# An eight-head hybrid attention block on one NeuronCore: half the search budget while splitting, another opening of attention, loads issued a job ahead

## The chip, the core and the metric

The kernel runs on one core of a Trainium2 chip. The metric is the device time of one execution in microseconds (us). TensorE is called PE here, its weight loads PEld, VectorE DVE, ScalarE ACT, GpSimd POOL and SyncE SP. Each engine runs its own list of instructions in order, and waits where an instruction needs something that another engine or a transfer has not delivered yet. All transfers (DMA) of this kernel are issued by SP, in the order of SP's list.

## The reference

One layer with 2048 positions and a width of 1024, in float32:

```python
xn = rms_norm(x, norm_gain)
proj = xn @ w_in                 # split into the inputs of both branches
# branch A: 8 heads of 64; a chunk of 64 sees itself and 8 chunks before it
yA = softmax(qc @ kc.T * scale + bias) @ vc * silu(gateA)
# branch B: 8 heads of 64 on one shared key and value; per block of 128 queries
score = sum_h relu(iq_h @ ik.T) * iw_h       # 8 indexer heads of 32
idx = top_k(score, 256)                       # among admissible keys
yB = softmax(q @ k[idx].T * scale) @ v[idx] * silu(gateB)
merged = sigmoid(gA) * (yA @ w_branch_a) + sigmoid(gB) * (yB @ w_branch_b)
out = rms_norm(x + merged @ w_out, final_norm_gain)
```

## The kernel before

Products of float32 matrices are made of three matmuls (`mm3`, L216): both operands are split into a high and a low part, and high x high, high x low and low x high are added up. So each product also costs splits: ACT writes the high part, DVE or POOL subtracts it to get the low part.

The program runs in these stages.

- **Scaling and index projection** (0 to about 100 us). x is normalized, and the inputs of the indexer are made. For two of the four groups of 512 positions the scaling runs later, beside the projection: `norm_early` loads two tiles (`xs`, and for one group `xa`), scales them on ACT and POOL and stores them.
- **Projection** (to about 1060 us). A list of `jobs` takes one piece of weights and one group of positions each. A job is two or four chains of 24 matmuls into a PSUM tile `acc`. The weights' splits (`wt`, L207 and L208) are made by ACT and POOL, the evacuations by ACT and DVE. The second half of the positions is finished by quarter products of sums of blocks, whose prepared weights come from `prep_full`.
- **Search** (within the projection, to 753 us). For branch B the positions' top 256 keys are found by thresholds, in order to get masks (`mskD`). `logits()` makes the scores of a block of 128 queries: a matmul into a buffer `lg` (L478), Relu on ACT (L480), weighted sum on DVE into `sc` (L485). `search()` finds the threshold of a pair of blocks by counting on DVE and ACT. Both are threads that yield with a cost in ns. After each chain of the projection `tick(x)` lets them run for `rate * x` ns, where the rate is one of `PUMP` and `PUMP2`. While `again` holds work that splits the second half's input, x is `TQ` or 0.35 instead of 1 or 0.5. When the threads have ended, `close_search` calls `search_again`: it counts the blocks whose count is off into `bad` (L577), adds that up on PE (L580) and makes a flag (L582), on which DVE and POOL branch. Then the pools of the sums are opened, and `again` gets their loads.
- **Attention** (about 1050 to 1885 us). A unit of branch A, `a_unit(G, h)`, is one head for a group of 512 queries; a unit of branch B, `b_unit(b, u)`, is two heads of block b. Each has loads, a first part (scores `s` on PE, L905 and L1014, maximum `mx` on DVE, L831, exponential on ACT, L909 and L1017) and a second part (transposes `pt` on PE, their split `pth` and `ptl`, product `O`). `attention()` runs the second part of a unit in turns with the first part of the next, and issues loads two units ahead. `seq` is the order of the units; it is made before by a rule that compares the shares of both branches' costs (`CA_`, `CB_`) that are done. `kv_at` says at which unit keys and values of a group of branch B (`kBt`, `vBt`) are loaded, and `extra` when the products `d` with `w_branch_a` and `w_branch_b` are made (`branch`).
- **Output product** `po` (L1420) to the end at 2087 us.

A scheduler that estimates times orders the instructions of each engine when the program is built, so a change of a rate or of the order of units moves instructions on all engines. The order that it made is fixed at run time.

## Time and profile before

| what | before |
|---|---|
| runs | 2090.68, 2093.07, 2093.47 us; median 2093.07 |
| profiled execution | 2089.03 us, span 2087.2 us |
| busy share | PE 96%, PEld 81%, DVE 71%, ACT 62%, POOL 39% |
| mean granted clock of PE | 0.987 |
| PE busy in 0 to 60 us | 49.21 of 60 |
| PE busy in 60 to 120 us | 47.49 of 60 |
| PE busy in 1060 to 1120 us | 43.68 of 60 |
| PE busy in 2040 to 2087 us | 38.87 of 47 |

Times of windows and rows are microseconds from the start of the span. A row of an instruction has its start, its length, engine, line and operation, output and inputs with partitions and elements, and in brackets how long the engine stood idle before it and what ended that. A row of a group has busy time, mean length in ns and idle time before it with its releasers. In a row of the table of waits stand the waiting and the releasing group. A granted clock of 1.00 is full speed.

### The profile page before, as it was taken

The numbers are of one execution on the slowest core, as the hardware profiler recorded it, in microseconds if no ns is written. First come the engines' busy times: TensorE is split into PE (matmuls) and PEld (weight loads), VectorE is DVE, ScalarE is ACT, GpSimd is POOL, SyncE is SP. The second block draws the span as 40 slices with busy tenths as digits, with TensorE's granted clock in tenths as the row PEclk, the third lists the DMA queues.
The fourth block names the chain that finished last, engine by engine and source line by source line (L and its number), as shares of the span: only waits on it lengthen the run. The fifth ranks groups of instructions, "written<-read, shape, count | busy, mean of one in ns | idle before, by whom it ended". The sixth has DMA issues, their size and how long they took to land.

```text
span 2087.2 us, 33654 instructions
## 1 busy us (share of the span) xinstructions
PE 1997.9 (96%) x10706; PEld 1693.9 (81%) x10706; DVE 1475.8 (71%) x3746; ACT 1285.5 (62%) x2644; POOL 809.9 (39%) x981
## 2 busy tenths in 40 slices
PE   8798999999998999999978999999999999999998
PEld 7576888889888887888867888888888888888886
DVE  6739899989798836555546678766886688865434
ACT  5465666656565544654458779866886688873221
POOL 2146322122221345545435455445444644343410
PEclk9899999999999999999989999999999999999999
DMA  9487433354545453333485664555245631145642
GB/s 359 145 290 242 166 131 123 106 176 147 178 170 175 150 184 112 116 129 119 134 237 171 203 192 143 155 177 191 88 124 178 195 109 51 58 140 191 216 134 91
DMA packets 225928, 333.77 MB, mean 160 GB/s; under 512 B 28625, under 2 KB 99665, under 8 KB 225617
## 3 DMA queue, kind: packets, MB, share of 16 engines
q1 hardware_dynamic: 225744, 331.57, 49.2%
q8 instruction: 85, 1.39, 0.3%
q14 instruction: 99, 0.80, 0.1%
HBM read 219.33 MB, written 112.16 MB: 159 GB/s over the span
## 4 chain that ended last, share of the span: by engine, by line
PE 53%; DMA 4%; DVE 2%; ACT 2%; issue 1%; POOL 1%; SPq 1%; DVEq 0%; ACTq 0%; POOLq 0%
PE acc L216 12%; PE po L1420 9%; PE d L216 8%; PE O L1039 6%; PE s L1014 5%; PE pt L1031 5%; PE O L949 3%; PE s L905 3%; PE pt L939 3%; DMA dst<-wA 1%; DMA kk<-kA 1%; DMA dst<-wB 1%; DVE P L831 1%; DMA ost<-wO 1%; DVE ptl L855 0%
## 5 line engine op out<-in xcount | busy, mean ns | idle before, releaser
L216 PE MATMUL acc<-xh,wt 128*128 128x512 f32 x1856 | 599.3, 394 | 5.7 <-DVE e L336 2.4
L216 PEld LDWEIGHTS acc<-xh,wt 128*128 128x128 f32 x1856 | 347.2, 188 | 84.4 <-DVE e L336 2.6
L216 PE MATMUL acc<-xl,wt 128*128 128x512 f32 x928 | 363.8, 393 | 0.0
L208 POOL TENSOR_TENSOR wt<-wst,wt 128x512 fp32r<-128x512 f32 (+1 forms) x108 | 145.4, 1375 | 419.8 <-ACT wt L207 303.4
L852 POOL TENSOR_TENSOR ptl<-pf,pth 128x512 fp32r<-128x512 f32 (+1 forms) x144 | 179.6, 1247 | 178.0 <-ACT pf L848 128.4
L855 DVE TENSOR_TENSOR ptl<-pt,pth 128x512 fp32r<-128x512 f32 (+1 forms) x288 | 187.3, 660 | 45.0 <-ACT pth L854 42.5
L216 PEld LDWEIGHTS acc<-xl,wt 128*128 128x128 f32 x928 | 174.5, 188 | 38.7
L485 DVE SCALAR_TENSOR_TENSOR sc<-lg,iw,sc 128x512 f32<-128x512 f32 (+2 forms) x266 | 178.6, 678 | 26.1 <-ACT lg L480 21.9
L1014 PE MATMUL s<-kBt,qsB 128*128 128x512 f32 (+3 forms) x640 | 188.0, 385 | 1.3 <-DVE mx L831 0.9
L480 ACT ACTIVATE lg<-lg 128x512 f32<-128x512 f32 (+2 forms) x304 | 147.9, 521 | 44.5 <-PE lg L478 43.6
L854 ACT ACTIVATE pth<-pt 128x512 fp32r<-128x512 f32 (+1 forms) x288 | 159.3, 578 | 25.2 <-PE pt L939 11.5
L1017 ACT ACTIVATE P<-P,mx 128x128 f32<-128x128 f32 (+15 forms) x128 | 154.3, 1207 | 20.6 <-DVE mx L831 20.1
L1031 PE MATMUL pt<-ident,P 128*128 128x128 f32 x1088 | 164.4, 273 | 1.2 <-DVE ptl L855 0.6
L1039 PE MATMUL O<-pth,vBt 128*128 128x256 f32 x544 | 146.3, 288 | 3.2 <-ACT pth L854 1.4
L1039 PE MATMUL O<-ptl,vBt 128*128 128x256 f32 x544 | 145.8, 295 | 1.8 <-POOL ptl L852 1.2
L831 DVE CUSTOM_DVE_ANT_0 P<-s,mk,mx 128x512 f32<-128x512 f32 (+2 forms) x192 | 125.0, 651 | 29.8 <-PE s L1014 24.7
L1031 PEld LDWEIGHTS pt<-ident,P 128*128 128x128 f32 x1088 | 127.0, 140 | 10.5 <-DVE ptl L855 1.1
L1077 POOL TENSOR_TENSOR dw<-dst,dw 128x512 fp32r<-128x512 f32 x64 | 82.7, 1292 | 124.5 <-ACT dw L1076 122.7
L478 PE MATMUL lg<-ikT,iqT 128*128 128x512 f32 (+2 forms) x304 | 111.3, 378 | 18.0 <-DVE sc L485 17.9
L905 PE MATMUL s<-kk,qz 128*128 128x256 f32 (+2 forms) x464 | 113.8, 341 | 15.4 <-DMA kk<-kA 7.8
L533 ACT ACTIVATE jk<-sc,st 128x640 int8<-128x640 f32 (+6 forms) x49 | 71.2, 1453 | 84.3 <-DVE st L551 73.6
L1014 PEld LDWEIGHTS s<-kBt,qsB 128*128 128x128 f32 x640 | 102.9, 190 | 15.8 <-DVE mx L831 9.1
(286 smaller groups left out, 4738.9 us busy)
## 6 DMA issues: line engine op xcount, KB each, us to landing
wst<-wP SPq DMA_DIRECT2D x100, 256.0 KB
wst<-wS SPq DMA_DIRECT2D x56, 256.0 KB
kk<-kA SPq DMA_DIRECT2D x56, 256.0 KB
vs<-vA SPq DMA_DIRECT2D x56, 256.0 KB
qz<-qA SPq DMA_DIRECT2D x96, 128.0 KB
xrow<-x SPq DMA_DIRECT2D x16, 512.0 KB
vA<-eh SPq DMA_DIRECT2D x32, 256.0 KB
dst<-wA SPq DMA_DIRECT2D x32, 256.0 KB
```

What stands on the lines that cost most here:

```text
L216: nc.tensor.matmul(acc, a, b, start=(first and i == 0), stop=(last and i == n - 1), **({} if first and last else {"skip_group_check": True}))
L480: nc.scalar.activation(lg, lg, AF.Relu)
L485: nc.vector.scalar_tensor_tensor(o_, lg, wv, o_, op0=OP.mult, op1=OP.add)
L852: nc.gpsimd.tensor_tensor(lo, pf, f32(hi), op=OP.subtract)
L854: nc.scalar.activation(hi, src, AF.Copy)
L855: nc.vector.tensor_tensor(lo, src, f32(hi), op=OP.subtract)
L905: nc.tensor.matmul(s_ps[:, :w], q[:, m, j * 128:(j + 1) * 128], kk[:, ko:ko + w], start=(m == 0), stop=(m == 1))
L1014: nc.tensor.matmul(s_ps[:, :w], q[:, h, :], kBt[:, m, a:a + w], start=(m == 0), stop=(m == 1))
L1017: nc.scalar.activation(P[:, e, :n], P[:, e, :n], AF.Exp, bias=mx[:, e:e + 1], scale=-1.0, accum_out=st["sum"][:, (u % 2) * 2 + e:(u % 2) * ...
L1031: nc.tensor.transpose(pt[:, k, e, :], P[:, e, (kt + k) * 128:(kt + k + 1) * 128], ident)
L1039: nc.tensor.matmul(o_, vBt[:, kt + k, :], src[:, k, :], start=(kt + k == 0 and n_ == 0), stop=(kt + k == b and n_ == 1), skip_group_check= ...
L1420: nc.tensor.matmul(accs[t, hf], a, b[:, n_], start=(k == 0 and i == 0), stop=(k == KT - 1 and i == 2))
```

## The change

- The search's budget for each chain while `again` holds work falls from 0.75 to 0.5 (`TQ`) and from 0.35 to 0.25; a score of one column costs 1.25 instead of 1.11 in the threads' account; `PUMP2` rises from 9000 to 11000.
- The loads of `norm_early` go into a function of their own, `load_early`, which is called a job ahead; the first of them is at job 8 instead of 6 (`EN0`).
- Attention starts with three units of branch A's first group; the other five are mixed with blocks 4 to 7 of branch B, then blocks 0 to 3 come, then 8 to 15 (`LEAD`, `GB`, `C0_`). The new order is A0.0 A0.1 A0.2 b4.0 A0.3 b4.1 A0.4 b4.2 A0.5 b4.3 b5.0 A0.6 b5.1 A0.7 b5.2 A1.0 and so on; the end is the same. Keys and values of groups 0 and 1 are loaded at the first unit, and the small copies on POOL that hold a load back (`GATE`) are made for groups 2 and 3 alone.
- The three bias tiles of heads `NB` and above are loaded behind the first unit instead of in `open_late`.
- `open_early` opens the pool `dna` ahead of `wp_`, which gives their tiles other addresses.

```diff
--- before.py
+++ after.py
@@ -38,14 +38,15 @@
 ROUNDS = 2
 SGB, TYB = 1, 1
 BLOCKS = [2, 4, 5, 6, 7, 8, 9, 10, 11, 12, 13, 14, 15, 3]
-PUMP, PUMP2 = (5300, 4500), 9000
+PUMP, PUMP2 = (5300, 4500), 11000
 DVE_KINDS = ("qb", "va", "ka", "qa")
-EN0, TQ = 6, 0.75
+EN0, TQ = 8, 0.5
 SQD = (2,)
 FIRST = (2, 4)
 SB, HB = 2, 3
 WK, WAT = 5, 1
-SPL, LEAD = 96, 8
+SPL, LEAD = 96, 3
+GB, C0_ = (1, 0, 2, 3), 14
 CA_, CB_, TAILB = 26, 9, 260
 NEWTON, HALVES = 3, 2
 GATE, OFF = 1, 60.0
@@ -483,7 +484,7 @@
                             nc.vector.tensor_scalar(o_, lg, wv, 0.0, op0=OP.mult, op1=OP.add)
                         else:
                             nc.vector.scalar_tensor_tensor(o_, lg, wv, o_, op0=OP.mult, op1=OP.add)
-                        yield 120 + w * 1.11
+                        yield 120 + w * 1.25
             nc.vector.memset(sc[0:64, n - 64:n], OUT)
             nc.sync.dma_start(scD[b, :, :n], sc[:, :n])
             scores[b] = sc[:, :n]
@@ -780,8 +781,8 @@
     def open_early():
 
         nonlocal sml, wk, wy, wz, dna, wp_, pe
+        dna = dph.enter_context(pool("dna", side="right"))
         wp_ = dph.enter_context(pool("wp_", side="right"))
-        dna = dph.enter_context(pool("dna", side="right"))
         sml = ph.enter_context(pool("sml", bufs=4, side="right"))
         wk = ph.enter_context(pool("wk", bufs=2, side="right"))
         wy = ph.enter_context(pool("wy", bufs=2, side="right"))
@@ -800,7 +801,6 @@
         kBt = att.tile([128, 2, S], F32R, name="kBt")
         vBt = att.tile([128, NT, 128], F32R, name="vBt")
         mk01 = att.tile([128, 2, 256], BF16, name="mk01")
-        load_bias(range(NB, H), att)
         nc.vector.memset(mk01, 0.0)
         nc.vector.memset(mk01[0:64, 0, 64:128], FAR)
         nc.vector.memset(mk01[0:64, 1, 192:256], FAR)
@@ -1095,12 +1095,11 @@
             pass
 
     extra, kv_at = {}, {}
-    seq = [("a", 0, h) for h in range(H)]
-    ua = [("a", g, h) for g in range(1, NG) for h in range(H)]
-    ub = [("b", b, u) for b in range(4 * NG) for u in range(4)]
-    cost = {"a": lambda g: CA_, "b": lambda b: 2 * (b + 1) + CB_}
+    ua = [("a", g, h) for g in range(NG) for h in range(H)]
+    ub = [("b", 4 * g + j, u) for g in GB for j in range(4) for u in range(4)]
+    cost = {"a": lambda g: CA_ if g else C0_, "b": lambda b: 2 * (b + 1) + CB_}
     ta, tb = sum(cost["a"](g) for _, g, _ in ua), sum(cost["b"](b) for _, b, _ in ub) - TAILB
-    done, ta = [OFF, 0.0], ta + OFF
+    done, seq = [0.0, 0.0], [ua.pop(0) for _ in range(LEAD)]
     while ua or ub:
         if ua and (not ub or done[0] / ta < done[1] / tb):
             z = ua.pop(0)
@@ -1112,7 +1111,7 @@
     at = {z: i for i, z in enumerate(seq)}
     units = [a_unit(g, i) if m == "a" else b_unit(g, i) for m, g, i in seq]
     for g in range(NG):
-        kv_at[max(H - 2, at["b", 4 * g, 0] - KVO)] = g
+        kv_at.setdefault(max(0, min(at["b", 4 * z, 0] for z in range(g, NG)) - KVO), []).append(g)
         i = at["a", g, H - 1]
         for c in range(KT):
             extra.setdefault(i + AOF + c // ASP, []).append(("a", g, c))
@@ -1160,7 +1159,7 @@
             (nc.vector if t < 2 else nc.gpsimd).tensor_tensor(mts[t][:, 1, k:k + 2], mf, f32(mts[t][:, 0, k:k + 2]), op=OP.subtract)
 
     def load_kv(g):
-        if g and GATE:
+        if g > 1 and GATE:
             nc.gpsimd.tensor_copy(kBt[:, 0, g * 512:g * 512 + 1], shared["mx"][:, 0:1])
             nc.gpsimd.tensor_copy(vBt[:, 4 * g, 0:1], shared["mx"][:, 0:1])
         for a in range(2):
@@ -1177,7 +1176,10 @@
             if i + 2 < len(units):
                 units[i + 2][0]()
             if i in kv_at:
-                load_kv(kv_at[i])
+                for g in kv_at[i]:
+                    load_kv(g)
+            if i == 0:
+                load_bias(range(NB, H), att)
             g1 = units[i + 1][1]() if i + 1 < len(units) else iter(())
             g2 = un[2]()
             live = [g1, g2]
@@ -1203,13 +1205,21 @@
 
     again = []
 
-    def norm_early(g, k):
+    early_x = {}
+
+    def load_early(g, k):
 
         xs = tkl.tile([128, 2, 512], F32, name="xs", tag="xs", bufs=2)
         nc.sync.dma_start(xs, io["xT"][g][:, k::4, :])
+        xa = None
         if g == 2:
             xa = tkl.tile([128, 2, 512], F32, name="xa", tag="xa", bufs=1)
             nc.sync.dma_start(xa, xnD[3][k])
+        early_x[g, k] = xs, xa
+
+    def norm_early(g, k):
+
+        xs, xa = early_x.pop((g, k))
         e = nc.gpsimd
         for z in range(2):
             nc.scalar.activation(xs[:, z], xs[:, z], AF.Copy, scale=gcol[:, k + 4 * z:k + 4 * z + 1])
@@ -1282,8 +1292,8 @@
         kind, c2 = UNITS[u]
         wt, s_ = wcur[r_], SLOT[g]
         rate[0] = PUMP[kind in DVE_KINDS] if r_ < nu or kind == "va" else PUMP2
-        if EN0 <= i < EN0 + 16 and i % 2 == 0:
-            norm_early(3 - (i - EN0) // 8, (i - EN0) // 2 % 4)
+        if EN0 <= i < EN0 + 16:
+            (norm_early if i % 2 else load_early)(3 - (i - EN0) // 8, (i - EN0) // 2 % 4)
         for c in range(4 if kind == "va" else 2):
             acc = next_acc(i)
             if kind == "va":
@@ -1294,7 +1304,7 @@
                 busy = bool(again)
                 if again and c % 2 == 0:
                     again.pop(0)()
-                tick(0.35 if busy else 0.5)
+                tick(0.25 if busy else 0.5)
             else:
                 w_ = slice(c * 128, c * 128 + 128)
                 mm3(acc, [((wt[:, 0, k, w_], wt[:, 1, k, w_]), (xh[s_][:, k, :], xl[s_][:, k, :]))
```

The order of three places shows what the scheduler made of it. Names: `acc` are the projection's chains, `xh_`/`xl_` and `wt` their split operands, `lg` the scores.

PE, the last score matmuls of the search, before (behind the last of them stand 432 projection matmuls until the flag's):

```order
L478 MATMUL lg<-ikT,iqT 128x512
L216 MATMUL acc<-wt,xl_121 128x288
L216 MATMUL acc<-wt,xh_120 128x288 x2
L216 MATMUL acc<-wt,xl_121 128x288
L216 MATMUL acc<-wt,xh_120 128x288 x2
L216 MATMUL acc<-wt,xl_121 128x288
L478 MATMUL lg<-ikT,iqT 128x512
L216 MATMUL acc<-wt,xh_118 128x288 x2
```

The same place of the changed kernel (behind the last, 254 until the flag's):

```order
L479 MATMUL lg<-ikT,iqT 128x512
L217 MATMUL acc<-xl_123,wt 128x512
L217 MATMUL acc<-xh_122,wt 128x512 x2
L217 MATMUL acc<-xl_123,wt 128x512
L479 MATMUL lg<-ikT,iqT 128x512
L217 MATMUL acc<-xh_122,wt 128x512
L217 MATMUL acc<-xh_124,wt 128x512
L217 MATMUL acc<-xl_125,wt 128x512
L479 MATMUL lg<-ikT,iqT 128x512
```

The last scores moved behind the chains of 288 columns, into those of 512.

SP, the transfers ahead of attention, before: the queries and gates of the first blocks (`qsB`, `sgB`), the store of branch A's last queries (`qA`), a mask (`mk`), and further on the bias and the keys of group 0:

```order
L994 DMA qsB<-qB_72 128x8x128
L996 DMA sgB<-gBD_86 128x4x128
L994 DMA qsB<-qB_72 128x8x128
L996 DMA sgB<-gBD_86 128x4x128
L714 DMA qA_63<-eht 128x512
L1001 DMA mk<-mskD 128x384
```

```order
L666 DMA bres_12326<-bias 128x384
L666 DMA bres_12328<-bias 128x384
L666 DMA bres_12330<-bias 128x384
L1167 DMA kBt<-kB 64x2x512 x2
L1169 DMA vBt<-vB 128x512
L864 DMA qz_12104<-qA_60 64x512 x3
L868 DMA kk<-kA_64 128x512
```

The changed kernel:

```order
L994 DMA qsB<-qB_73 128x8x128
L996 DMA sgB<-gBD_87 128x4x128
L1001 DMA mk<-mskD 128x640
L994 DMA qsB<-qB_73 128x8x128
L715 DMA qA_63<-eht 128x512
L996 DMA sgB<-gBD_87 128x4x128
```

```order
L1166 DMA kBt<-kB 64x2x512 x2
L1168 DMA vBt<-vB 128x512
L1166 DMA kBt<-kB 64x2x512 x2
L1168 DMA vBt<-vB 128x512
L864 DMA qz_12104<-qA_60 64x512 x3
L868 DMA kk<-kA_64 128x512
L667 DMA bres_12382<-bias 128x384
L667 DMA bres_12384<-bias 128x384
L667 DMA bres_12386<-bias 128x384
```

The store `qA<-eht` moved ahead of the second `sgB`; keys and values of group 1 came ahead of the third unit's queries and keys (`qz`, `kk`), and the bias went behind them.

PE, the fourth unit of attention, before (`s` are scores, `pt` transposes, `O` products with the values):

```order
L949 MATMUL O<-pth,vs 128x512
L939 MATMUL pt<-ident,P 128x128 x2
L905 MATMUL s<-kk,qz_12104 128x128 x2
L905 MATMUL s<-kk,qz_12104 128x256 x2
L939 MATMUL pt<-ident,P 128x128 x3
L905 MATMUL s<-kk,qz_12104 128x384 x2
L939 MATMUL pt<-ident,P 128x128 x5
L905 MATMUL s<-kk,qz_12104 128x128 x2
L905 MATMUL s<-kk,qz_12104 128x384 x2
L949 MATMUL O<-ptl,vs 128x512
```

The changed kernel:

```order
L939 MATMUL pt<-ident,P 128x128 x5
L905 MATMUL s<-kk,qz_12104 128x128 x2
L905 MATMUL s<-kk,qz_12104 128x384 x2
L949 MATMUL O<-pth,vs 128x512
L1014 MATMUL s<-kBt,qsB 128x384 x2
L1014 MATMUL s<-kBt,qsB 128x256 x2
L978 MATMUL pt<-ident,rb 128x128 x4
L939 MATMUL pt<-ident,P 128x128 x3
L1014 MATMUL s<-kBt,qsB 128x384 x2
L939 MATMUL pt<-ident,P 128x128 x7
```

Scores of branch B's block 4 (`s<-kBt,qsB`) now stand between the transposes of branch A's units, where scores of another unit of branch A stood.

## The prediction

> **What bounds the kernel now.** I read the page's busy shares first, then the stretches of the span, then the table of waits, and last the single instructions around the places that the change touches.
>
> ```profile
> span 2087.2 us, 33654 instructions
> PE 1997.9 (96%) x10706; PEld 1693.9 (81%) x10706; DVE 1475.8 (71%) x3746; ACT 1285.5 (62%) x2644; POOL 809.9 (39%) x981
> 793.65 250.20 PE acc L216 x1081
> ```
>
> PE is busy for 96% of the span: 89 us are idle, and no edit takes a matmul away, so all that can be won is idle time and the time in which PE runs slower than full speed. The third row is a stretch with nothing in its way: 1081 matmuls of 512 columns in 250.20 us, 0.2315 us each, the pace used below. The stretches (columns: window, length, busy of PE, PEld, DVE, ACT, POOL, granted clock, DMA share, GB/s) show where PE loses it.
>
> ```profile
> 470.00:480.00 10.00, 7.99 (x55) 7.66 (x54) 9.74 (x22) 6.86 (x16) 5.78 (x5) 0.92 0.49 159
> ...
> 555.00:577.00 22.00, 22.00 (x97) 17.82 (x96) 14.82 (x52) 13.68 (x18) 5.09 (x4) 1.00 0.62 213
> ...
> 601.00:626.00 25.00, 25.00 (x109) 20.27 (x109) 24.99 (x37) 14.85 (x29) 7.57 (x5) 1.00 0.57 193
> 626.00:651.00 25.00, 17.72 (x107) 16.08 (x106) 24.69 (x34) 13.53 (x30) 8.66 (x5) 0.86 0.60 200
> ...
> 1060.00:1120.00 60.00, 43.68 (x233) 38.65 (x232) 31.13 (x118) 39.06 (x106) 21.84 (x24) 0.80 0.73 206
> 1120.00:1180.00 60.00, 55.34 (x343) 47.97 (x342) 40.20 (x123) 46.85 (x127) 32.92 (x39) 1.00 0.66 198
> 1180.00:1240.00 60.00, 59.36 (x380) 51.91 (x379) 44.54 (x133) 46.93 (x106) 33.46 (x34) 1.00 0.59 182
> ```
>
> The table of waits gives for each the sum, the count and the longest, in us:
>
> ```profile
> PE lg L478 <- DVE sc L485: 17.9, 12, 3.7
> PE s L905 <- DMA kk<-kA: 7.8, 3, 4.8
> PE s L905 <- DVE mx L831: 7.2, 6, 5.3
> PE acc L216 <- DVE part L1361: 2.3, 2, 1.5
> PE acc L216 <- DVE wt L1279: 1.3, 2, 0.8
> ```
>
> Three places matter. At 470 and at 626 a score matmul (L478) waits for DVE to free a score buffer; DVE is then full (24.99 of 25 and 24.69 of 25 us), while at 555 it does 14.82 of 22. At 1060 the attention opens: PE is busy for 43.68 of 60 us at a clock of 0.80, and waits for keys (`kk`) and for the first maxima (`mx`).  Everything later runs at 59 of 60.
>
> **The search's stalls.** The change halves the budget of the search while `again` holds splits (0.75 to 0.5, 0.35 to 0.25) and prices a score column at 1.25 instead of 1.11. No instruction is added. In the order of PE, 25 score matmuls stood between the 1992nd and the 2110th projection matmul, with none in the 172 ahead of them; now 11 stand in those 172. That is where DVE had the 7 us of slack of the 555 row. Price of the 626 stretch: 25 − 17.72 = 7.28 idle, and the busy part ran at 0.86, so 0.14 × 17.72 = 2.5 slow; 9.8 in all. I take −8 (0 to −9.8): most of a stall goes when its work spreads over a stretch with slack, but the score stream still has places where five matmuls stand together. The 470 stretch loses 2.0 idle and 0.08 × 7.99 = 0.6; I take −2 (0 to −2.6), by the same share.
>
> **The flag.** `search_again` ends the search: DVE makes `bad`, PE adds it up (L580), DVE makes the flag.
>
> ```profile
> 669.82 0.40 PE L478 MATMUL lg<-ikT,iqT 128*128 128x512 f32 x1
> 732.59 0.08 DVE L577 DVE_READ_ACCUMULATOR bad<-bad 128x1 f32 x1
> 753.74 0.19 PE L580 MATMUL lg<-ones,bad 128*1 128x1 f32 x2
> 753.96 0.14 DVE L582 TENSOR_SCALAR flag<-lg 1x1 int32<-1x1 f32 x1 [19.92 <-PE lg L580]
> ```
>
> From the last score matmul to `bad` the search needs 732.67 − 669.82 = 62.9 us; PE came to the flag after 83.9, so DVE waited 19.92 for PE, and PE for nobody. The order of before puts 432 projection matmuls between the two, 168 of them with 288 columns; the changed order puts 254 there, all with 512. 254 × 0.2315 = 58.8, less than 62.9: the cover is gone and PE waits 62.9 − 58.8 = 4.1 at the flag. Queued behind it on PE are the projection matmuls. I take +4. The bounds are 0, if DVE, which has fewer other evacuations there, runs the tail a few us faster, and +9, if score work that is late lengthens it by 5.
>
> What could shorten the tail is a DVE instruction that is held up while POOL works:
>
> ```profile
> 680.70 5.09 POOL L208 TENSOR_TENSOR wt<-wst,wt 128x512 fp32r<-128x512 f32 x4 [41.78 <-ACT wt L207]
> 680.76 1.28 DVE L548 TENSOR_SCALAR sm<-sm 128x2 f32<-128x2 f32 x1
> 687.92 0.16 DVE L548 TENSOR_SCALAR sm<-sm 128x2 f32<-128x2 f32 x1
> 717.16 7.14 POOL L208 TENSOR_TENSOR wt<-wst,wt 128x512 fp32r<-128x512 f32 x4 [15.90 <-ACT wt L207]
> ```
>
> The same line of DVE takes 1.28 us while POOL splits weights and 0.16 when it does not. The tail of before has three such bursts of POOL, the changed order two and the end of one. If a burst holds DVE up all along, a missing one of 5.09 us gives the tail more than the 4.1 back that PE would wait: a rival below, at 0. If it costs DVE one instruction, the row gives 1.28 − 0.16 = 1.1, and 3 of the 4.1 stay.
>
> The Trainium skill, "SBUF — State Buffer", section "SBUF: two separate sides", has a rule for this: GpSimd and VectorE share a pair of ports as an exclusive lock, and the loser stands still until the other's instruction has ended. By that rule the 1.28 is a wait, which the trace bears out with its 0.16 beside it, and the tail would lose one such wait for each instruction of POOL that goes; the sum would come out up to 4 us lower than mine.
>
> **After the flag.** `close_search` opens the pools of the sums, and their loads, splits and the first quad's weights follow. Between the flag and the first use of those weights stood 120 projection matmuls and stand 92 now: 28 × 0.2315 = 6.5 us less cover for the same chain of DMA, ACT, DVE. Before, that chain was already a little late:
>
> ```profile
> 784.27 0.73 PE L216 MATMUL acc<-xh,wt 128*128 128x512 f32 x2 [0.49 <-DVE wt L1279]
> 786.00 0.73 PE L216 MATMUL acc<-xh,wt 128*128 128x512 f32 x2 [0.77 <-DVE wt L1279]
> ```
>
> Since it is late already, cover that is lost shows up as waiting, apart from what a wait at the flag gives DVE and POOL in time to prepare. I take +5 (0, if DVE is freer, to +9, the 6.5 with a slow clock behind it). The waits on `wt` and `part` of 1.3 and 2.3 would grow by that.
>
> **The opening of attention.** Before: eight units of branch A's first group, then b0.0 and so on. Now A0 is mixed with blocks 4 to 7 (A0.0, A0.1, A0.2, b4.0, A0.3, b4.1, ...), keys and values of both first groups (1.5 MB) are loaded at once, and three loads of bias (192 KB each) go behind the first unit instead of ahead of everything. Counts per engine stay the same apart from three gate copies on POOL that become two and two split packs, under 1 us.
>
> ```profile
> L909 ACT ACTIVATE P<-P,mx 128x512 f32<-128x512 f32 x8 | 5.8, 722 | 2.7 <-DVE mx L831 2.7
> L854 ACT ACTIVATE pth<-pt 128x512 fp32r<-128x512 f32 x39 | 22.4, 596 | 2.3 <-PE O L949 0.8 <-PE pt L1031 0.8 <-PE pt L939 0.5
> L1017 ACT ACTIVATE P<-P,mx 128x640 f32<-128x640 f32 x8 | 6.7, 832 | 1.3 <-DVE mx L831 1.3
> ```
>
> The single instructions of PE at the opening, and the transfers that they hang on (start, length):
>
> ```profile
> 1066.31 1.33 PE L905 MATMUL s<-kk,qz 128*128 128x384 f32 x4 [5.27 <-DVE mx L831]
> 1078.17 1.19 PE L905 MATMUL s<-kk,qz 128*128 128x128 f32 x4 [4.82 <-DMA kk<-kA]
> ...
> 1056.85 2.13 SPq L996 DMA_DIRECT2D sgB<-gBD  x1
> 1059.08 5.04 DMA qA<-eht
> 1071.34 6.69 DMA kk<-kA
> ```
>
> What the three windows lose is 16.32 + 4.66 + 0.64 = 21.6 idle and 0.20 × 43.68 = 8.7 slow: 30.3 us, the most that this edit can win. A unit of b4 (two exponentials of 0.832, 1.66, and copies of 0.596) asks of ACT about as much against PE's time as a unit of A0 (four exponentials up to 0.722 and the same copies), so by ACT alone the mix is no lighter. What it brings is independent work: at 1060 ACT is busy for 39.06 of 60 us, the waits (5.27 for `mx`, 4.82 for `kk`) stand in a chain of one kind of unit, and from 1120, where both kinds are mixed, ACT does 46.85 and 46.93. If the first 60 us reach that pace, ACT's 39.06 + 46.85 of work fit in about 85.91 / 46.9 × 60 = 110 us instead of 120: −10. Added to it is the first chain on SP: `qA<-eht` was issued behind both `sgB` loads (2.13 each) and goes ahead of the second now: −2. The slow clock lifts with the idle time; a quarter of 8.7 is −2. Sum −14. The bounds are −25 (30.3 less the 4.82 for `kk`) and 0: the third unit's `kk` (6.69 us) stands behind 1.5 MB of keys and values now, instead of 0.75 MB and 0.58 MB of bias, which at 206 GB/s would take 0.8 us longer, and the first three units are A0 in both orders. −14 lies near the middle, by the row of 1120, which has the mix and still loses 4.66.
>
> **No effect.** Early loads of scaling (`load_early`, EN0 8): the order of POOL is the same in its first 304 instructions and SP's in its first 226, and the `xs` loads stand in the same places; 0. The pools `dna` and `wp_` change places: addresses alone; 0.
>
> **The sum:** −8 − 2 + 4 + 5 − 14 = −15. The profiled execution took 2089.0 (2087.2 and 1.8 around the span): 2074. The median of the runs, 2093.07, is 4.0 above that execution: **2078 us**. Added up, the low ends give −37 (2056) and the high ends +18; they will not all fall on one side, so the main case's own range is 2068 to 2088.
>
> **The rivals.**
>
> *The tail is short enough:* POOL's missing burst removes the wait at the flag, 0 instead of +4: 2074. For it the 1.28 against 0.16; against it that POOL's other split work moves too. 0.14.
>
> *The opening gains all:* −25 for −14 and no wait at the flag: 2078 − 11 − 4 = 2063. For it: the windows from 1180 on show that the mix can run at 59.36 of 60. Against it: b4 needs as much ACT per unit. 0.18.
>
> *The opening gains nothing:* ACT and the first transfers set it in both orders. −8 − 2 + 4 + 5 = −1: 2092, no change that can be told. For it: the first three units and their `kk` are the same. Against it: ACT has 21 us idle in the first 60. 0.17.
>
> *Slower: the search ends later than its flag.* The last score matmul moves by 83.9 − 58.8 + 6.5 = 31.6 us of PE time towards the end. If DVE, full in two of the windows shown, has not caught up, half of that, 15, becomes waiting at the flag, with PE's clock 0.20 down for some 20 us behind it, as at 1060 (4), and the 626 stall is not gained but moved: 0 − 2 + 15 + 4 + 5 − 14 = +8: 2101. It decides when wait and slow clock at the flag pass 2 − 5 + 14 = 11 us. Against it: the 19.92 us that DVE stood waiting at L582, and DVE's idle 7 us at 555. 0.15.
>
> **How the numbers follow.** The main case holds 0.36. A measurement of this kernel tells about 0.2%, 4.2 us. Below 2088.9 lie the main case, the short tail and the full opening: 0.68 faster; the opening without gain gives 0.17 within it; 0.15 slower. The range goes from 2058, some 5 below the full opening and near the sum of the low ends, to 2098; beyond it lies most of the slower case.
>
> **What would show it.** Right: no wait of `lg` on `sc` over 3 us near 630; PE waiting some 4 us on `bad` at the flag; waits on `wt` and `part` near 785 of 5 us together; ACT over 45 of 60 us in the first window of attention, PE over 50. Wrong: a wait of over 11 us at the flag, a new stall of `lg` on `sc` elsewhere, or the third unit still waiting 5 us for `kk` and the first window still at 44 of 60.

## The result, and the profile after

The changed kernel takes 2104.61 us (median of 6 runs, 2100.2 to 2109.4) against 2093.27 us before (6 runs, 2090.68 to 2096.13). The ratio is 1.0053, with an interval of 1.0035 to 1.0070: it is slower by 11 us, where 15 us faster were forecast.

The page of the changed kernel begins so:

```profile
span 2098.4 us, 33634 instructions
PE 2005.5 (96%) x10706; PEld 1693.7 (81%) x10706; DVE 1460.3 (70%) x3746; ACT 1286.2 (61%) x2644; POOL 803.1 (38%) x979
```

The work is the same and PE's share too, so the 11 us must be found by place. Equal times of the two kernels hold different work. Therefore I cut both traces at equal amounts of PE work: each form of matmul counts with its usual distance from start to start (the 35th percentile of that form in the two traces), all of them make some 1900 us, and a stretch runs from one sum of work to another. What a stretch loses is its length less its work. With the matmuls weighted a little otherwise, most cells move by about 1 us and those of e17's opening and the stretch behind it by 2 to 3. The table gives how much longer than before each stretch takes, in us. "Start" is up to 420 us of work, "470" and "640" hold the two stalls of the score matmuls, "after flag" is the rest of the projection (720 to 990), "opening" attention's first 120 us of work (990 to 1110), "behind" the next 150 (to 1260), "long" the next 390 (to 1650), and "end" the last 120 (to 1770) of attention. The runs e1 and so on are told below.

| kernel | start | 470 | 640 | after flag | opening | behind | long | end |
|---|---|---|---|---|---|---|---|---|
| changed | +1.2 | -3.8 | +3.1 | +2.0 | -9.1 | +13.4 | +0.2 | +3.7 |
| e1 opening of before | +1.4 | -3.2 | +4.6 | +2.9 | -3.5 | +1.3 | -2.4 | +0.8 |
| e2 search of before | +3.7 | +2.1 | +2.1 | -0.6 | -9.7 | +15.3 | -0.5 | +4.9 |
| e4 fast search | +4.3 | -3.2 | +2.7 | -3.6 | -8.1 | +14.8 | -0.3 | +3.1 |
| e8 opening of before, fast search | +2.0 | -3.2 | +3.2 | -3.1 | -3.5 | +0.3 | -1.3 | +1.2 |
| e9 = e8 and mix | +1.0 | -3.8 | +3.9 | -2.2 | -9.9 | +3.5 | 0.0 | +0.9 |
| e10 = e8 and block order | +0.3 | -3.8 | +3.6 | -2.9 | -8.9 | +14.7 | -4.7 | +0.3 |
| e15 = e10 and mix | +1.2 | -3.8 | +3.2 | +0.4 | -8.0 | +12.3 | -5.5 | +2.2 |
| e17 = e9 and new pacing | +2.0 | -3.8 | +3.0 | -3.6 | -3.2 | +5.2 | -2.8 | +4.4 |
| e18 = e9 and old price | +1.4 | +0.5 | +0.7 | -2.7 | -9.4 | +4.3 | -0.1 | -0.2 |

So the opening does gain 9 us, and the stretch behind it loses 13. In the windows of attention, cut at these places (columns as in the prediction: window, length, PE, PEld, DVE, ACT, POOL, granted clock, DMA share, GB/s), before has:

```profile
1056.30:1226.10 169.80, 147.40 (x877) 128.34 (x877) 109.32 (x351) 125.67 (x321) 80.51 (x89) 0.93 0.66 196
1226.10:1391.90 165.80, 164.48 (x1081) 145.98 (x1080) 123.14 (x345) 133.74 (x273) 85.53 (x83) 1.00 0.53 161
```

and the changed kernel:

```profile
1058.80:1219.50 160.70, 144.23 (x894) 125.50 (x893) 109.69 (x339) 123.32 (x283) 73.23 (x75) 0.95 0.60 179
1219.50:1398.70 179.20, 168.61 (x1058) 145.36 (x1057) 122.89 (x359) 135.95 (x311) 92.92 (x96) 1.00 0.58 177
```

Before, PE was idle for 22.4 and 1.3 us in the two, now it is for 16.5 and 10.6. No other engine is full in the second: ACT does 136 of 179 us. The table of waits for that stretch shows what is late (sum, count, longest). Its first row before is

```profile
PE s L905 <- DVE mx L831: 0.4, 1, 0.4
```

and the changed kernel's first three are

```profile
PE d L217 <- ACT dw L1076: 3.9, 4, 2.4
PE pt L1031 <- DVE ptl L855: 1.4, 3, 1.0
PE d L217 <- DVE mx L831: 1.1, 2, 0.8
```

The branch products `d` wait for their weights' split `dw`. Before, no wait for `dw` stands in that table. These are 3.9 of the 10.6 us; the rest is spread over waits of 1.4 us and less.

Only a part of the opening's gain stands at the waits that were named for it. Its first 60 us in the changed kernel, begun 3.7 us behind the cut as the row from 1060 was before, and the third unit's wait for its keys are

```profile
1062.50:1122.50 60.00, 47.25 (x278) 41.27 (x277) 37.27 (x133) 44.05 (x112) 24.86 (x28) 0.86 0.68 192
```

```profile
1081.33 1.19 PE L905 MATMUL s<-kk,qz 128*128 128x128 f32 x4 [6.46 <-DMA kk<-kA]
```

The longest waits of the whole opening are, before and then changed,

```profile
PE s L905 <- DMA kk<-kA: 7.8, 3, 4.8
PE s L905 <- DVE mx L831: 6.6, 4, 5.3
PE d L216 <- ACT dw L1076: 3.3, 2, 2.9
```

```profile
PE s L905 <- DMA kk<-kA: 6.5, 1, 6.5
PE s L905 <- DVE mx L831: 5.7, 5, 4.3
```

The flag, of which I expected a new wait, has none. In the changed kernel (start, length; the last of the three is PE's):

```profile
701.75 0.40 PE L479 MATMUL lg<-ikT,iqT 128*128 128x512 f32 x1
...
758.20 0.09 DVE L578 DVE_READ_ACCUMULATOR bad<-bad 128x1 f32 x1
...
760.96 0.19 PE L581 MATMUL lg<-ones,bad 128*1 128x1 f32 x2
```

PE came to the flag 59.2 us after the last score matmul (58.8 were worked out from the order), but `bad` was there after 56.5, where before it took 62.9. The stall near 640, which I expected to go, grew:

```profile
626.00:651.00 25.00, 15.08 (x86) 13.49 (x85) 25.00 (x36) 10.98 (x25) 4.18 (x4) 0.80 0.49 168
```

```profile
635.01 0.49 PE L479 MATMUL lg<-ikT,iqT 128*128 128x512 f32 x1 [2.44 <-DVE sc L486]
642.01 1.45 PE L479 MATMUL lg<-ikT,iqT 128*128 128x512 f32 x2 [6.50 <-DVE sc L486]
```

Ahead of it the stream of scores has a gap, which ends later than before. The scores on both sides of the gap are, before,

```profile
554.05 0.34 PE L478 MATMUL lg<-ikT,iqT 128*128 128x384 f32 x1
...
594.08 1.32 PE L478 MATMUL lg<-ikT,iqT 128*128 128x512 f32 x5
```

and in the changed kernel

```profile
564.66 0.34 PE L479 MATMUL lg<-ikT,iqT 128*128 128x384 f32 x1
...
619.54 1.33 PE L479 MATMUL lg<-ikT,iqT 128*128 128x512 f32 x5
```

### The profile page after: what moved, and what is told of

Its sections match the earlier page's. It is cut to its first block, busy times and chain, and to the rows that moved or that the text cites. A ratio compares the mean times of both kernels' runs of the same rounds, so it can differ in the third digit from the quotient of the medians.

```text
span 2098.4 us, 33634 instructions
## 1 busy us (share of the span) xinstructions
PE 2005.5 (96%) x10706; PEld 1693.7 (81%) x10706; DVE 1460.3 (70%) x3746; ACT 1286.2 (61%) x2644; POOL 803.1 (38%) x979
## 4 chain that ended last, share of the span: by engine, by line
PE 67%; DMA 11%; DVE 7%; POOL 6%; ACT 4%; issue 3%; SPq 1%; another core or an unknown queue 0%; DVEq 0%; POOLq 0%; ACTq 0%
PE acc L217 26%; PE po L1430 7%; PE d L217 6%; PE O L1039 5%; PE s L1014 5%; PE pt L1031 5%; DMA wst<-wS 4%; PE O L949 3%; PE s L905 3%; PE lg L479 2%; PE pt L939 2%; PE xa L217 2%; DMA mf<-mD 1%; DVE P L831 1%; POOL wst L1284 1%
## 5 line engine op out<-in xcount | busy, mean ns | idle before, releaser
L209 POOL TENSOR_TENSOR wt<-wst,wt 128x512 fp32r<-128x512 f32 (+1 forms) x108 | 136.6, 1294 | 433.8 <-ACT wt L208 407.0
L1017 ACT ACTIVATE P<-P,mx 128x640 f32<-128x640 f32 (+15 forms) x128 | 154.6, 1210 | 21.3 <-DVE mx L831 20.7
L905 PE MATMUL s<-kk,qz 128*128 128x256 f32 (+2 forms) x464 | 111.2, 338 | 14.6 <-DVE mx L831 7.7
L479 PE MATMUL lg<-ikT,iqT 128*128 128x512 f32 (+2 forms) x304 | 105.7, 376 | 17.7 <-DVE sc L486 16.6
L909 ACT ACTIVATE P<-P,mx 128x640 f32<-128x640 f32 (+4 forms) x128 | 97.9, 765 | 26.1 <-DVE mx L831 25.0
```

What stands on the lines that cost most here:

```text
L479: nc.tensor.matmul(lg[:, :w], iqT[:, h, :], ikT[:, c0:c0 + w], start=True, stop=True)
L905: nc.tensor.matmul(s_ps[:, :w], q[:, m, j * 128:(j + 1) * 128], kk[:, ko:ko + w], start=(m == 0), stop=(m == 1))
L1017: nc.scalar.activation(P[:, e, :n], P[:, e, :n], AF.Exp, bias=mx[:, e:e + 1], scale=-1.0, accum_out=st["sum"][:, (u % 2) * 2 + e:(u % 2) * ...
```

## The experiments

Every ratio is to the kernel before, run beside it on the same chip; its interval is in brackets. Line numbers of some variants are one higher than those of the changed kernel.

**Which half costs the time (e1, e2).** In e1 the order of units, the key loads with their copies on POOL and the bias loads are put back (of the edit, the order alone is shown):

```diff
-    ua = [("a", g, h) for g in range(NG) for h in range(H)]
-    ub = [("b", 4 * g + j, u) for g in GB for j in range(4) for u in range(4)]
-    done, seq = [0.0, 0.0], [ua.pop(0) for _ in range(LEAD)]
+    seq = [("a", 0, h) for h in range(H)]
+    ua = [("a", g, h) for g in range(1, NG) for h in range(H)]
+    ub = [("b", b, u) for b in range(4 * NG) for u in range(4)]
+    done, ta = [OFF, 0.0], ta + OFF
```

> The changed kernel with the opening of attention as before (order of units, times of the key loads, bias loads ahead); the new search pace, the early loads and the swapped pools stay. In the traces of before and after, the 11 us come as +1.5 before 100 us, -4 at 470, +3 at 640, +1.8 up to 1060, then -9 at the opening of attention and +17 behind it. Theory 1, the order of attention's units costs the time: this kernel is within 3 us of the kernel before (2093 to 2096). Theory 2, the search pace does, by leaving other buffers and queues behind: it stays 7 us or more slower (2100 or more).

In e2 the search's pace is put back instead:

```diff
-EN0, TQ = 8, 0.5
+EN0, TQ = 8, 0.75
-                tick(0.25 if busy else 0.5)
+                tick(0.35 if busy else 0.5)
-                        yield 120 + w * 1.25
+                        yield 120 + w * 1.11
-PUMP, PUMP2 = (5300, 4500), 11000
+PUMP, PUMP2 = (5300, 4500), 9000
```

> The changed kernel with the search pace of before (0.75, 0.35, 1.11, 9000); the new opening of attention stays. Theory 1 (the order of attention's units): 7 to 9 us slower than before, 2100 to 2102, with the same pattern in attention: 9 less lost up to 110 us from its start, 13 to 17 more behind that. Theory 2 (the search pace): within 2 us of before or faster, down to 2084, since the opening's gain of 9 is kept.

e1: 2091.19 us, 1.0003 (0.9990 to 1.0016). e2: 2105.18 us, 1.0060 (1.0040 to 1.0079). Theory 1 holds: attention's part of the change, the order with its loads, costs the time, and the new pace is neutral in sum. The table shows both patterns: e1 is near 0 in "behind", e2 has +15.3 there.

**Block order by number (e3).**

```diff
-GB, C0_ = (1, 0, 2, 3), 14
+GB, C0_ = (0, 1, 2, 3), 14
```

> The changed kernel with blocks 0 to 3 beside branch A's first group and 4 to 7 behind them (the order of blocks by number), still mixed from the fourth unit on. Theory 1a, the short blocks 0 to 3 lose their time wherever they stand, and the change moved that loss from the opening to the middle: the opening loses more than in the changed kernel (by 5 to 9 us), the stretch from 140 to 400 us behind it 9 to 13 less; total 2098 to 2105. Rival 1b, the loss comes from the mix's new proportions (A units spread otherwise up to the end): the stretch from 140 us on keeps its 13 to 17, total 2104 or more.

2101.67 us, 1.0051 (1.0032 to 1.0070). "Opening" is at -5.1, "behind" at +10.9, "end" at +5.8. By place this speaks against 1a: with the natural order of blocks most of the loss stays, so the block order cannot be all of it. The total lies in 1a's range and below 1b's, so it does not decide. From the 21st to the 50th unit this order is that of before but for one swap of neighbours; behind that branch A's units come up to three places earlier.

**A search that isn't slowed (e4).**

```diff
-EN0, TQ = 8, 0.5
+EN0, TQ = 8, 1.0
-                tick(0.25 if busy else 0.5)
+                tick(0.5 if busy else 0.5)
```

> The changed kernel with no slowing of the search while splitting (1.0 and 0.5 in place of 0.5 and 0.25). In the changed kernel DVE did 37.7 of 60 us from 540 to 600 (before: 48.5), and was full from 601 to 651, where PE lost 13.2 us (before: 10.3). Theory, the slower pace built that backlog of DVE: the stall near 640 falls to 8 us or less, total 5 us or more below the changed kernel. Rival, the stall comes from splits of DVE that stand among the scores in any order: it stays at 10 to 13 us, total within 3 us of the changed kernel.

2098.23 us, 1.0036 (1.0019 to 1.0053). The stall near 640 stayed (+2.7 against +3.1), so the theory falls, although the total is as far below the changed kernel's as it said: the slower pace does not make that stall. The gain is at another place, "after flag" (-3.6 against +2.0); in total the two intervals overlap.

**The branch products' weights in halves (e5, e6).** The wait for `dw` at the products is tested with two halves of each tile and a buffer for each (the edit's first lines):

```diff
-        st = dn.tile([128, 4, 128], F32, name="dst", tag="dst", bufs=1)
-        wt = dn.tile([128, 2, 4, 128], F32R, name="dw", tag="dw", bufs=1)
+        for z in range(2):
+            st = dn.tile([128, 2, 128], F32, name="dst", tag=f"dsh{z}", bufs=1)
+            wt = dn.tile([128, 2, 2, 128], F32R, name="dw", tag=f"dw{z}", bufs=1)
```

> The changed kernel with the weights of the branch products (dst, dw) in two halves with a buffer each, so that the first half of the next product's weights can arrive while PE works on the second half; the products are the same. In the stretch that follows the opening (120 to 340 us behind the start of attention) PE loses 13 us more in the changed kernel than before, and 7 of these stand at the products d, 5.2 of them as idle time that mostly ACT's split of dw ends. Theory D, the weights' single buffer sets that: the idle time at d falls from 5.2 to 2 us or less there, total 5 us or more below the changed kernel (2099 or less). Rival, the products stand too close together and the idle time goes to the next thing that is late: d's share falls, the total stays within 2 us.

> The kernel before with the same halves of the branch products' weights. Control: its idle time at d in that stretch is 0.1 us, 3.3 at the opening and 2.0 later. Theory D: it gains at most 3 us, less than the changed kernel does. Rival (the halves help or cost both alike, by more or fewer transfers): the same difference as in the changed kernel, within 2 us.

e5: 2103.16 us, 1.0052 (1.0036 to 1.0068). e6: 2095.59 us, 1.0025 (1.0014 to 1.0035). In e5 the wait fell as theory D has it; the row of that stretch is now

```profile
PE d L217 <- ACT dw L1078: 0.6, 1, 0.6
```

and "behind" fell from +13.4 to +8.2. But "opening" rose from -9.1 to -5.8, 640 from +3.1 to +4.7 and the second half of "long" by 2, and the total is that of the changed kernel. With a buffer for each half that wait is nearly gone, and the time does not come back: the rival holds for the total. The control gained 6.5 in the opening and lost 9 elsewhere. The order of the whole program is another with the two transfers, so that a single place cannot be judged by the total.

**The end (e7).**

```diff
-CA_, CB_, TAILB = 26, 9, 260
+CA_, CB_, TAILB = 26, 9, 180
```

> The changed kernel with the share of branch B that is kept for the end cut from 260 to 180, so that the last unit of branch A stands at place 88 as in the kernel before (86 in the changed kernel) and seven units of branch B, not nine, run alone at the end. PE loses 6.1 us before and 9.8 in the changed kernel in the last 100 us of attention's work. Theory E, the two units more that run alone at the end cost those 3.7: it falls to 7 or less there, total 2 to 4 us below the changed kernel. Rival: the end keeps 9 to 10 us, no change in total.

2101.78 us, 1.0059 (1.0041 to 1.0077). "End" fell from +3.7 to +2.1 and the last part of "long" by 5, and "behind" rose from +13.4 to +17.4. No gain in total, by the ratio.

**Opening of before with the fast search (e8).** The edits of e1 and e4 together.

> The opening of attention as before, with no slowing of the search while splitting (1.0 and 0.5), the price 1.25 and the rate 11000 of the change. With the changed attention the faster search lost nothing at the preparation after the flag (3.9 us otherwise) and as much near 640 (13.2). Theory, search and attention act apart: the 4 us of the stall at 470 stay gone, the 3.9 after the flag go too, 3 us more are lost near 640: 3 to 6 us below the kernel before, 2086 to 2090. Rival, they trade against each other: within 2 us of before.

2084.85 us, 0.9972 (0.9961 to 0.9982): faster than both kernels, and a little below what was expected. The theory holds by place: -3.2 at 470, -3.1 after the flag, +3.2 near 640. Some 3.5 us more come at the opening, as in e1, with the order of before in both; what brings them is not shown. e1 and e8 differ by the slowing alone, and their intervals do not overlap (1.0003 and 0.9972): slowing the search costs some 6.5 us here, 6.0 of it after the flag.

One reading of why "after flag" gains: PE reaches the flag at 750.4 us in e8, before at 753.7, in the changed kernel at 761.0, so the preparation has more projection beside it. The waits behind the flag until attention are, before,

```profile
PE acc L216 <- ACT part L1342: 1.8, 1, 1.8
PE acc L216 <- DVE part L1361: 1.5, 1, 1.5
PE acc L216 <- DVE wt L1279: 1.3, 2, 0.8
```

in the changed kernel

```profile
PE acc L217 <- DVE part L1371: 1.5, 1, 1.5
PE acc L217 <- ACT wt L1288: 0.8, 2, 0.6
PE acc L217 <- ACT wv L1288: 0.8, 2, 0.6
PE acc L217 <- DVE wv L1289: 0.6, 1, 0.6
PE acc L217 <- DVE wt L1289: 0.4, 1, 0.4
```

and in e8

```profile
PE acc L217 <- DVE part L1371: 1.5, 1, 1.5
PE acc L217 <- DVE part L1355: 0.3, 1, 0.3
```

They sum to 4.6, 4.1 and 1.8 us. So they go with the gain of e8, but they do not explain the changed kernel's +2.0.

**The parts of the new order, one by one on e8 (e9 to e11).** e9 mixes the first group alone (its first key loads come earlier with it), e10 changes the block order (with the times of the key loads and the copies on POOL), e11 makes the bias loads late alone:

```diff
+    mix = [z for j in range(5) for z in (("b", j // 4, j % 4), ("a", 0, 3 + j))]
+    seq[3:13] = mix
```

> The kernel with the opening of before and the fast search (the run before this one, 0.9972 of before), and in it only the last five units of branch A's first group mixed with b0.0 to b1.0; from the 14th unit on the order of units is that of before word for word. Theory M, the mixing of the first group takes its gain from what follows, since the branch products of the first group, which filled the opening, are then made five units later: the opening loses 3 to 6 us less, the stretch behind it 8 to 10 more, total 4 us or more above its base (2089 or more). Rival P, the new proportions behind the opening cost the time and not the mix: it is as fast as its base or faster (2080 to 2086).

```diff
-    ub = [("b", b, u) for b in range(4 * NG) for u in range(4)]
+    ub = [("b", b, u) for b in (4, 5, 6, 7, 0, 1, 2, 3, 8, 9, 10, 11, 12, 13, 14, 15) for u in range(4)]
```

> The same base with the blocks in the order of the change (4 to 7, then 0 to 3, then 8 to 15) and the changed times of the key loads, but all eight units of branch A's first group ahead and the pacing of before. Theory M: within 3 us of its base (2082 to 2088), since nothing of the first group is mixed. Rival B, the longer blocks in the opening and the shorter ones in the middle cost the time: 5 us or more above its base, lost in the stretch of blocks 0 to 3.

```diff
-        load_bias(range(NB, H), att)
+            if i == 0:
+                load_bias(range(NB, H), att)
```

> The same base with only the three bias loads behind the first unit, as in the change. Theories M, P and B: within 2 us of its base, at the opening 0 to 3 us less lost. Rival L, the loads push the transfers of the units behind them back: 4 us or more above its base.

e9: 2082.55 us, 0.9967 (0.9953 to 0.9980). e10: 2087.07 us, 0.9982 (0.9972 to 0.9992). e11: 2083.31 us, 0.9971 (0.9960 to 0.9982). Against e8's 0.9972 the mix and the late bias cost nothing; theory M falls and L too. The mix gains 6.4 at the opening and gives 3.2 of it back. The block order is some 2 us slower than e8, less than rival B's 5, and inside the intervals. But it has the pattern of the changed kernel in full: -8.9, then +14.7, and then -4.7. Its waits in "behind" are

```profile
PE d L217 <- ACT dw L1077: 6.5, 3, 3.2
```

One product of e10 shows the chain (start, length, idle before):

```profile
1285.86 1.28 POOL L1078 TENSOR_TENSOR dw<-dst,dw 128x512 fp32r<-128x512 f32 x1
...
1287.60 0.44 SPq L1075 DMA_DIRECT2D dst<-wB  x1
1287.96 2.13 PEld L217 LDWEIGHTS d<-yb,dw 128*128 128x128 f32 x10
1287.99 2.54 PE L217 MATMUL d<-yb,dw 128*128 128x512 f32 x10
1292.68 0.63 ACT L1077 ACTIVATE dw<-dst 128x512 fp32r<-128x512 f32 x1 [2.48 <-DMA dst<-wB]
...
1293.36 0.74 PE L217 MATMUL d<-yb,dw 128*128 128x512 f32 x2 [2.04 <-ACT dw L1077]
```

The buffer `dst` is single, so here the next weights are fetched only when POOL has read the last ones (1287.14). The transfer ends some 5 us after its issue, ACT's half takes 0.63, and PE's product is over after 2.5 us. From the issue to the end of ACT's half are 5.7 us, and a product of 12 matmuls fills 2.8 of them: PE needs about 3 us of other work before the next product, an estimate from these rows, and less stands in its list there: it idles for 2.04.

**Splits on POOL (e12).**

```diff
-        nc.vector.tensor_tensor(lo, f32(lo), f32(hi), op=OP.subtract)
+        (nc.vector if early_ else nc.gpsimd).tensor_tensor(lo, f32(lo), f32(hi), op=OP.subtract)
```

> The same base with the subtraction of the second half's input splits on POOL instead of DVE until the search has ended. Near 640 PE loses 13.3 us in the base, while DVE does search, scores and these splits (0.7 us each) without a pause and POOL is mostly idle. Theory S, DVE's load sets that stall: it falls by 4 us or more, total down by as much (2081 or less). Rival, the splits arrive later from the slower engine and PE waits for them: the stall stays or PE waits for xl instead, total within 2 us or above.

2086.09 us, 0.9983 (0.9969 to 0.9997). The stall near 640 is at +4.3 against e8's +3.2: moving the splits does not help, as the rival has it. It does not clear DVE's load, though. In e12's windows DVE is as full as ever from 601 to 651 without the splits, while it has 25 us free in the 68 before:

```profile
533.00:601.00 68.00, 68.00 (x297) 55.43 (x296) 43.10 (x109) 38.24 (x63) 14.37 (x12) 1.00 0.50 176
601.00:651.00 50.00, 40.06 (x201) 34.09 (x200) 49.45 (x73) 26.59 (x53) 30.07 (x23) 0.90 0.53 171
```

POOL is busy for 30.07 us there against 13.69 in e8, and the same small subtraction of DVE (L551, two columns) takes 0.737 us on average against 0.402. So e12 did not relieve DVE in that stretch, and theory S stays open.

**Products spread over units (e13, e14).** On e10 and on the changed kernel:

```diff
-PH, AOF, ASP, BSP = 2, 1, 2, 4
+PH, AOF, ASP, BSP = 2, 1, 2, 1
```

> The run with the block order of the change alone (ratio 0.9982), with branch B's products behind a group made one per unit over eight units instead of four per unit over two. With four per unit, group 1's eight products fall among b7.2 to b0.1, and 11.3 of the 30.5 us that PE loses in that stretch stand at d. Theory C, the eight products, each behind its own weights, have too little other work beside them there: the stretch falls to 24 or less, total 5 us or more faster. Rival, short blocks lose it themselves: d's share falls, s, O and pt take it, the stretch stays at 27 to 31.

> The changed kernel with the same spreading of branch B's products. Theory C: the stretch from 120 to 270 us of attention's work falls from 29.1 by 5 or more, total 2099 or less. Rival: the stretch stays within 2 us, total 2102 to 2106.

e13: 2085.91 us, 0.9981 (0.9968 to 0.9994). e14: 2099.58 us, 1.0046 (1.0029 to 1.0063). "Behind" stays at +14.6 and +14.0, with waits of the same size at the same products (1.8 and 2.8 us where e10 has 2.0 and 3.2). The edit hardly moved the products there. I read that as the chain above setting their pace, not the unit at which they are called. So e13 does not test theory C; that there is too little other work beside them is read from the rows of e10 and not shown by a run.

**Pacing (e15, e17) and what can be joined (e16).** e15 has block order and mix of the change with the pacing of before; e17 puts the pacing of the change on e9; e16 joins e9 and e11. The main lines of e17's edit are

```diff
-    seq = [("a", 0, h) for h in range(H)]
-    done, ta = [OFF, 0.0], ta + OFF
+    done, seq = [0.0, 0.0], [ua.pop(0) for _ in range(LEAD)]
```

> The run with the block order alone, and in it also the first group's last five units mixed with b4.0 to b5.0, as in the change; the pacing from there on is that of before. Against the changed kernel it differs in attention by the pacing alone (and the early bias). In the last 390 us of attention's work before the output the changed kernel loses 31.8 us and the block order alone 24.6. Theory T, the pacing costs these 7: it loses 26 or less there, total 2083 to 2089. Rival, the mix costs it: 30 or more there, total 2092 or more.

> The mix alone (0.9967) with the bias loads late (0.9971 alone); both stand on the fast search with the opening of before (0.9972). If their gains at the opening, 6.3 and 1.7 us, add up and nothing is given back: 2079 to 2082. If the opening is at its limit by then: 2082 to 2085.

> The mix alone (ratio 0.9967), with the pacing of the change for all units: three units of the first group ahead, the others by a cost of 14 each, no offset of 60; blocks in their natural order, bias early, fast search. The order of units differs from the mix by a few places only: the first group ends four units later, and the first branch's units after that come a unit earlier or later. Theory T, the pacing costs 5 us or more: 2088 or more, lost in the stretch behind the opening (19.3 in the mix alone) and at the end (6.9). Rival: within 3 us of the mix alone, 2080 to 2086.

e15: 2091.69 us, 0.9999 (0.9986 to 1.0012). e17: 2091.87 us, 1.0000 (0.9989 to 1.0012). e16: 2083.54 us, 0.9968 (0.9955 to 0.9981). e4 differs from e15 by the pacing and the late bias: 1.0036 against 0.9999. e17 differs from e9 by the pacing and by leaving out POOL's copies for group 1: 1.0000 against 0.9967. So the pacing is worth some 7 us by two pairs, with one small companion in each. The late bias may not be free beside the new pacing: e3 has the order of units of e17 word for word, and differs by the slowed search and the late bias; it is at 1.0051 against 1.0000, 10.7 us, where the slowing alone is worth 3.6 (changed against e4) to 6.5 (e1 against e8). No run tries the late bias alone in that order.

The stretch with the 31.8 us of the expectation is that from 1500 to 1770 of work (270 us, not the 390 written there); e15 loses 26.2 in it, so theory T holds there by a hair and its total lies at the rival's edge. In e17 the 7 us are lost at the opening (-3.2 against -9.9) and at the end (+4.4 against +0.9), not behind the opening as expected. With the matmuls weighted otherwise 2 to 3 us of the opening's part fall behind it, so this division is not sure. e16 is no faster than e9: the opening's gains do not add up.

**The price of a score (e18).** On e9:

```diff
-                        yield 120 + w * 1.25
+                        yield 120 + w * 1.11
```

> The mix alone with the price of a score column at 1.11 instead of 1.25, the rate 11000 and the fast search kept. If the price removed the stall at 470 (4.9 before, 1.2 to 1.9 with the price): 4 or more are lost there again, total 3 us above the mix alone (2085 or more). If the rate did: it stays at 2 or less, total within 2 us.

2084.27 us, 0.9968 (0.9955 to 0.9980). The stall at 470 is back (+0.5 against -3.8), and the one near 640 is smaller (+0.7 against +3.9). The price moves the loss from one to the other and is worth nothing that can be told. The windows say how. DVE's work from 533 to 601 is, before, changed and in e18 (a row of each, in this order):

```profile
533.00:601.00 68.00, 68.00 (x296) 55.20 (x295) 55.07 (x139) 40.21 (x61) 14.09 (x12) 1.00 0.51 176
```

```profile
533.00:601.00 68.00, 68.00 (x296) 55.34 (x296) 44.16 (x107) 38.33 (x61) 10.13 (x8) 1.00 0.51 179
```

```profile
533.00:601.00 68.00, 68.00 (x296) 55.19 (x295) 55.21 (x134) 40.20 (x61) 15.81 (x12) 1.00 0.52 174
```

With the higher price DVE leaves 11 us more of this stretch unused, whether the search is slowed (44.16) or not (42.09 in e9, on which e18 stands; e8 and e12, 43 both), and has the work behind it, where it is full. e2 has the old price too: DVE does 55.31 us there, and PE waits for `sc` for 7.2 us between 610 and 680, in e18 for 7.3, before for 7.3, in the changed kernel for 9.9.

## Why the prediction was wrong

By ratios along a line of kernels, the change falls apart so: before 1.0000; price, rate and fast search with the opening of before (e8) 0.9972; block order (e10) 0.9982; mix (e15) 0.9999; pacing and late bias (e4) 1.0036; slowed search (changed) 1.0053. In us of 2092 these steps are -5.9, +2.1, +3.6, +7.7, +3.6. Each has an uncertainty of 2 to 5 us, so only the first and the fourth are well clear of it. The fast search is faster than that of before, and the early loads and the pools come in with the first step.

The table tells attention apart from the rest: the sum of its last four columns is -3.3 in e8, +1.4 in e10, +1.0 in e15, +9.5 in e4 and +8.2 in the changed kernel. So the block order costs some 5 us in attention, the mix nothing (the step of e15 stands in "after flag", +0.4 against -2.9, and no run tells why), and the pacing with the late bias 8.5. From e9 to e17 the same sum goes from -5.5 to +3.6.

- **The opening, -14, failed.** The place gained 9.1, inside the bounds of 0 to -25, but only in part by what was said. -3.5 of it stands in e1 and e8 too, with the order of before. Of the signs named, PE should have been busy for over 50 of the first 60 us of attention and ACT for over 45, and the third unit should not have waited 5 us for `kk`. The rows above have 47.25, 44.05 and a wait of 6.46. At `s` PE waits 2.2 us less, while 3.3 at the branch products are gone from the opening and waits for `dw` stand behind it instead. The step that failed is "Everything later runs at 59 of 60": the sum ended at 1240 us and took the rest for untouched. The runs showed in its place +13.4 in the next 150 us of work and +3.7 at the end, so attention as a whole lost 8. The rule that makes `seq` was in the diff (three units ahead, a cost of 14, no offset), and the forecast costed the mix of the first units and neither the pacing, worth some 7 us by two pairs of runs, nor the block order, worth some 5 in attention. The branch products were not costed in their new surroundings either: no row of before had a wait at them there. Why the stretch behind loses 13 is shown by place and order (e10 has +14.7 with the block order), and not by mechanism: with the wait for `dw` gone, e5 is no faster in total.
- **The stall at 626, -8, failed in sign:** +3.1. The step that failed is "That is where DVE had the 7 us of slack". I counted 11 score matmuls that did come earlier (of the 25 of before, 18 stand there by the 2110th projection matmul and the rest by the 2184th), and not the gap behind them, which ends at 619.54 instead of 594.08: of DVE's work 10.9 us less was done in the slack (55.07 to 44.16). e18 shows the price of 1.25 as the cause: in the table's kernels with the fast search and that price this cell is between +2.7 and +3.9, in e18 +0.7. The slowing, which I blamed first, is not (e4).
- **The stall at 470, -2:** right in sign, -3.8 with all its neighbourhood. It goes with the price and not with the slowing (-3.2 in e4, +0.5 in e18), and it is paid for near 640.
- **The flag, +4:** there was no wait. PE's side was right (58.8 against 59.2), DVE's tail was 6.4 us shorter. The rival with the missing burst of POOL forecast this result, but the traces bear out only a part of its reason. In the tail of before eight small instructions of DVE take 1.01 to 1.30 us during POOL's bursts, in the changed kernel six take 1.13 to 1.23, where 0.16 is usual; the search's 122 instructions take 43.3 us before and 40.6 now. The larger part is the reason of the term's lower bound, fewer evacuations: DVE does 28 instructions of them in the tail before, 13.2 us, and 8 now, 5.5 us. How much of the 6.4 each brought is not shown by a run.
- **After the flag, +5:** +2.0 in the changed kernel, and -3.1 in e8, where the flag comes 10.5 us earlier than in the changed kernel. The mechanism, that the preparation needs cover behind the flag, is borne out by e1 and e8, but the waits behind the flag are 4.1 us in the changed kernel and 4.6 before, so its +2.0 is not shown to come from them. The size was too high by 3.
- **No effect, 0:** the late bias costs nothing (e11). Pools and early loads stand in every variant and were not tried alone; with both in and the slowed search, e1 is at 1.0003.
- **The rivals:** the slower one had another mechanism, a search that ends later than its flag, and a time of 2101, near the measured 2105 for a wrong reason. The rival in which the opening gains nothing is refuted by place: the opening gained 9, some 5 to 6 of it beyond e1 and e8.

## What to carry to other kernels

Where a list of units is planned ahead, a change of its first units changes what stands beside everything later, so cost it to the end of the stage. Cut both traces at equal work, not at equal times: windows by the clock hold different work in the two kernels, and here a gain of 9 us was given back within the next 150. And where a fixed engine list holds a chain such as transfer, split, product with one buffer, ask for each new place how much other work stands between two links: here, by the rows of e10, 2.8 us of product need some 3 us beside them.

## What the runs showed of the hardware that was not expected

The first 60 us ran at different granted clocks, though PE's list is the same in both kernels there: changed and before,

```profile
0.00:60.00 60.00, 49.27 (x262) 42.86 (x263) 36.99 (x89) 36.08 (x74) 13.54 (x112) 0.94 0.86 326
```

```profile
0.00:60.00 60.00, 49.21 (x274) 42.75 (x275) 37.28 (x89) 35.76 (x74) 13.98 (x112) 1.00 0.86 325
```

Of 20 kernels, 8 show 0.94 or 0.95 there, 3 show 0.97 and 9 show 1.00. In that time PE did 262 against 274 matmuls. What this is worth further on is not shown: at 0.94 the changed kernel has +1.2 in the column "start", and e1, at 1.00, has +1.4. One profile of each kernel cannot tell whether it belongs to the kernel or to the execution.
